# Decay exponents as products in PSUM: one change to a hybrid RG-LRU and gated-DeltaNet block on one core

## The chip, the cores and the metric

The kernel runs on one core of one Trainium2 chip. The core has a matrix engine (TensorE, PE in the profile), three engines for elementwise work (VectorE or DVE, ScalarE or ACT, GpSimd or POOL), and SyncE (SP), from whose queue this kernel issues its DMAs. Matrix products land in PSUM, eight banks of 128 partitions by 512 numbers of four bytes; everything else lies in SBUF, and large arrays in DRAM. The metric is device time in microseconds (us) of one execution, the median of several runs.

## The reference, cut to what matters

Two layers run over a context of 256 tokens and a latent stream of 256 tokens, with 1024 features. Layer 0 mixes with a bidirectional RG-LRU, layer 1 with a bidirectional gated DeltaNet; each is followed by a SwiGLU feed-forward part. The change lies in the DeltaNet. It has 8 query and key heads, 16 value heads of 128 numbers each, and two directions. Per chunk of tokens, head and direction it computes:

```python
gc = jnp.cumsum(gc, axis=-1)
diff = gc[..., :, None] - gc[..., None, :]
decay = jnp.where(incl, jnp.exp(jnp.where(incl, diff, 0.0)), 0.0)
kb = kc * bc[..., None]
m = jnp.where(strict, jnp.einsum('bhid,bhjd->bhij', kb, kc) * decay, 0.0)
rhs = jnp.concatenate([vc * bc[..., None], kb * jnp.exp(gc)[..., None]], axis=-1)
sol = lax.linalg.triangular_solve(m, rhs, left_side=True, lower=True, unit_diagonal=True)
u, w = sol[..., :d_v], sol[..., d_v:]
v_new = u - jnp.einsum('bhcd,bhde->bhce', w, s)
attn = jnp.where(incl, jnp.einsum('bhid,bhjd->bhij', qc, kc) * decay, 0.0)
o = (jnp.einsum('bhcd,bhde->bhce', qc * jnp.exp(gc)[..., None], s)
     + jnp.einsum('bhij,bhje->bhie', attn, v_new))
g_last = gc[..., -1]
s = (s * jnp.exp(g_last)[..., None, None]
     + jnp.einsum('bhcd,bhce->bhde', kc * jnp.exp(g_last[..., None] - gc)[..., None], v_new))
```

`q` and `k` are normalised per token and head, `beta` (`bc`) is a sigmoid, `g` a negative softplus. The kernel uses chunks of 128 tokens where the reference uses 64; the result of the recurrence doesn't depend on that.

## The kernel before

**An order made by a planner.** The kernel's text is not the order in which engines work. A `Recorder` takes every operation with a cost (`_cost`), the engines that could do it, and the tiles it reads and writes. `flush` then plays the engines forward by these costs: of what is ready it takes the lowest priority number (place in the text plus a `bias` for its stage), gives out buffers first in, first out, puts an operation with two possible engines on the one that ends it first, and issues the operations in that order. So all instructions carry line 576, the one that calls them, and groups of the profile are told apart by their tiles. Each engine then works strictly in the order it was given.

**Products.** A weight comes as a 128 by 1024 tile `raw` (3 buffers) by a DMA on SP. It is split into a rounded part `whi` and a rest `wlo` in the F32R type, and each product is three matmuls (`mm3`). Plain F32 matmuls show as two records each.

**The DeltaNet stages.** The 16 value heads go in four groups `g` of four value heads, that is two key heads. `TUNE["prog"]` lists the stages in order:

- A(h), `stage_a`: products for key, two value heads and query of head h; convolution (`cu`), SiLU, transposes, the norms `rk2`, spills of keys and values to DRAM.
- E(g), `stage_e`: the decays of a group in the tile `gn`: 32 matrices of 128 by 128, one for each of 4 chunks, 2 directions and 4 heads. One DMA of 2 MB broadcasts rows of the cumulated gates (`rows`, in DRAM) to all partitions; 8 selects on POOL put -1e30 or 1e30 on one side of the diagonal; 32 exponentials on ACT add the column's part as a bias.
- N(g), `stage_n`: `gn` times minus beta (`nbt`), times the products of keys with keys (`ps_g`), and then the inverses of the 32 by 32 diagonal blocks of all 32 matrices at once, on DVE (`lw`, `lmul`): 30 steps of two instructions and some transposes.
- L(g), `stage_l`: merging of the blocks' inverses to the inverse of 128 by 128, with matmuls of 32 rows (`ps_w1`, `ps_z`) and then of 64 (`ps_w2`, `ps_z2`), both kinds shown without their digit. Its `first` and `second` run over both directions and both halves: all of `first`, then all of `second`.
- P(g), `stage_p`: for each key head a broadcast `qg` of 0.5 MB, selects to `at`, exponentials of both, `at` times beta and the product of keys and queries (`ps_kq`), and `qg` times the query.
- C(g), `stage_c`: the recurrence over four chunks for both directions: `ps_ks`, `r`, `ps_y`, `yy`, `ps_s`, the state `S`, and in the last two steps the outputs `ps_o`, a sum of two products in PSUM (`qg` with `S`, `at` with `yy`), gathered in `oa`.
- Z and W: products for the output gate, gating, and the first part of the output projection.

PSUM is given out by tags: two banks `mm` for products, one `ta` for stage A, two `tr` for `ps_g`, `ps_kq` and all merges, three `st` for C. `gn` has two buffers, so E(g+2) waits for C(g).

Lines that matter: `PROG` and `TUNE` 72 to 74, `_cost` 259, `add_any` 321, `flush` 387, the gates' setup 1155 to 1201, E at 1272, N 1291, L 1344, `first` and `second` 1400 and 1412, P 1433, C 1480, the loop over the stages 1642.

## Time and profile before

| What | us |
|---|---|
| median of 3 runs (lowest, highest) | 1427.63 (1426.83, 1431.89) |
| the profiled execution | 1428.36 |
| its span, first to last instruction | 1426.6 |
| PE busy in it | 1308.5 |
| DVE busy | 1092.5 |
| ACT busy | 590.2 |
| POOL busy | 293.0 |
| DMA | 208.26 MB, a mean of 146 GB/s |

Layer 0 and its feed-forward part take the span up to some 640 us, the DeltaNet with its output projection the stretch to about 1205, and the last feed-forward part the rest. Busy time is the time in which an engine ran at least one instruction. Matmuls overlap, so the mean duration of one is longer than the distance to the next. The granted clock tells which share of TensorE's full clock it had.

### The profile page before, as it was taken

The numbers are of one execution on the slowest core, as the hardware profiler recorded it, in microseconds if no ns is written. First come the engines' busy times: TensorE is split into PE (matmuls) and PEld (weight loads), VectorE is DVE, ScalarE is ACT, GpSimd is POOL, SyncE is SP. The second block draws the span as 40 slices with busy tenths as digits, with TensorE's granted clock in tenths as the row PEclk, the third lists the DMA queues.
The fourth block names the chain that finished last, engine by engine and source line by source line (L and its number), as shares of the span: only waits on it lengthen the run. The fifth ranks groups of instructions, "written<-read, shape, count | busy, mean of one in ns | idle before, by whom it ended". The sixth has DMA issues, their size and how long they took to land.

```text
span 1426.6 us, 23481 instructions
## 1 busy us (share of the span) xinstructions
PE 1308.5 (92%) x9195; PEld 1126.8 (79%) x9195; DVE 1092.5 (77%) x1843; ACT 590.2 (41%) x1119; POOL 293.0 (21%) x273
## 2 busy tenths in 40 slices
PE   6999999899999999999868999799578899899997
PEld 3667768778888888897757889689577899899997
DVE  5889976777777776468699849869789777777775
ACT  3267863333334332025594453663543731211100
POOL 2000010100121110123566433623421320000000
PEclk9999999999999999999979979969669899899998
DMA  9544433355555554344752403603703215455563
GB/s 359 192 153 165 156 118 103 137 181 188 203 190 178 178 188 148 96 139 132 181 173 89 147 33 114 189 31 105 177 1 79 87 46 207 134 187 183 176 187 111
DMA packets 69791, 208.26 MB, mean 146 GB/s; under 512 B 6960, under 2 KB 14384, under 8 KB 69424
## 3 DMA queue, kind: packets, MB, share of 16 engines
q1 hardware_dynamic: 69680, 206.77, 45.7%
q8 instruction: 72, 1.18, 0.3%
q14 instruction: 39, 0.32, 0.1%
HBM read 196.71 MB, written 10.03 MB: 145 GB/s over the span
## 4 chain that ended last, share of the span: by engine, by line
PE 62%; issue 16%; DVE 11%; DMA 6%; ACT 3%; SPq 2%; POOL 0%; POOLq 0%; DVEq 0%; ACTq 0%
PE ps_mm L576 34%; PE ps_dn L576 9%; PE ps_g L576 4%; PE ps_ada L576 3%; PE ps_wo L576 2%; PE ps_z L576 2%; PE ps_o L576 2%; SPq L576 2%; PE ps_y L576 2%; DVE lw L576 2%; PE ps_w L576 2%; DVE cu L576 2%; DMA raw<-dn_w_in 1%; DMA spill<-on 1%; DMA kspill<-k 1%
## 5 line engine op out<-in xcount | busy, mean ns | idle before, releaser
L576 PE MATMUL ps_mm<-hh,whi 128*128 128x512 f32 (+1 forms) x888 | 330.8, 373 | 14.3 <-DVE cu L576 7.8
L576 PE MATMUL ps_mm<-hh,wlo 128*128 128x512 f32 (+1 forms) x888 | 327.1, 369 | 6.7 <-DVE wlo L576 4.6
L576 PE MATMUL ps_mm<-hl,whi 128*128 128x512 f32 (+1 forms) x888 | 326.2, 368 | 2.0 <-DVE hl L576 2.0
L576 DVE TENSOR_TENSOR wlo<-raw,whi 128x1024 fp32r<-128x1024 f32 (+2 forms) x189 | 233.3, 1234 | 26.4 <-ACT whi L576 18.3
L576 DVE CAST whi<-raw 128x1024 fp32r<-128x1024 f32 (+1 forms) x168 | 115.2, 686 | 143.6 <-PE ps_mm L576 69.2
L576 PEld LDWEIGHTS ps_mm<-hh,whi 128*128 128x128 f32 x888 | 172.3, 194 | 50.6 <-issue 9.6
L576 PEld LDWEIGHTS ps_mm<-hh,wlo 128*128 128x128 f32 x888 | 171.9, 194 | 36.1 <-DVE wlo L576 6.3
L576 PEld LDWEIGHTS ps_mm<-hl,whi 128*128 128x128 f32 x888 | 172.1, 194 | 26.6 <-DVE hl L576 2.2
L576 POOL TENSOR_TENSOR wlo<-raw,whi 128x1024 fp32r<-128x1024 f32 x49 | 118.7, 2423 | 234.5 <-ACT whi L576 101.4
L576 PE MATMUL ps_dn<-fh,whi 128*128 128x256 f32 (+1 forms) x374 | 122.7, 328 | 0.0
L576 PE MATMUL ps_dn<-fl,whi 128*128 128x256 f32 (+1 forms) x374 | 122.5, 328 | 0.0
L576 PE MATMUL ps_dn<-fh,wlo 128*128 128x256 f32 (+1 forms) x374 | 122.3, 327 | 0.0
L576 PE MATMUL ps_mm<-h2h,whi 128*128 128x256 f32 x352 | 100.8, 287 | 1.1 <-ACT h2h L576 1.1
L576 PE MATMUL ps_mm<-h2h,wlo 128*128 128x256 f32 x352 | 100.7, 286 | 0.4 <-DVE wlo L576 0.4
L576 PE MATMUL ps_mm<-h2l,whi 128*128 128x256 f32 x352 | 100.7, 287 | 0.0
L576 ACT ACTIVATE whi<-raw 128x1024 fp32r<-128x1024 f32 (+1 forms) x70 | 71.6, 1023 | 66.4 <-PE ps_mm L576 33.0
L576 ACT ACTIVATE fh<-sg 128x256 fp32r<-128x256 f32 (+1 forms) x43 | 22.4, 522 | 143.4 <-DVE sg L576 142.0
L576 POOL TENSOR_TENSOR x<-x,ring 128x1024 f32<-128x1024 f32 x13 | 34.3, 2635 | 212.6 <-ACT ring L576 212.6
L576 PEld LDWEIGHTS ps_dn<-fh,whi 128*128 128x128 f32 x374 | 71.1, 190 | 6.8 <-issue 0.4
L576 PEld LDWEIGHTS ps_dn<-fh,wlo 128*128 128x128 f32 x374 | 71.1, 190 | 6.2 <-DVE wlo L576 0.2
L576 PEld LDWEIGHTS ps_dn<-fl,whi 128*128 128x128 f32 x374 | 71.1, 190 | 5.9
L576 DVE SCALAR_TENSOR_TENSOR cu<-ps_mm,sm,cu 128x510 f32<-128x510 f32 (+2 forms) x96 | 64.9, 678 | 8.8 <-ACT cu L576 6.7
(301 smaller groups left out, 2735.3 us busy)
## 6 DMA issues: line engine op xcount, KB each, us to landing
ring<-ada_w SPq DMA_DIRECT2D x96, 512.0 KB, 4.5
raw<-ffn_gu SPq DMA_DIRECT2D x88, 512.0 KB, 3.7
raw<-dn_w_in SPq DMA_DIRECT2D x49, 512.0 KB, 3.7
raw<-ffn_down SPq DMA_DIRECT2D x34, 512.0 KB, 3.6
raw<-rg_w_in SPq DMA_DIRECT2D x16, 512.0 KB, 3.7
gn<-rows SPq DMA_DIRECT2D x4, 2048.0 KB, 16.3
raw<-ffn_down SPq DMA_DIRECT2D x17, 384.0 KB, 3.3
raw<-dn_w_out SPq DMA_DIRECT2D x12, 512.0 KB, 3.9
```

The lines of the kernel that those rows point to most:

```text
L576: call(*[real(x) for x in args], **{n: real(v) for n, v in kw.items()})
```

## The change

Decays. The broadcasts, the selects and the multiplication by beta go. In their place, the exponent of a whole decay matrix is summed up in a PSUM bank by three F32R products, for four heads at once: a column part (cumulated gate of the column, with the logarithm of beta in it), a row part, and a triangle of -1e30. One exponential reads the bank and writes the decay. Numbers are split in an F32R part and a rest, which lie in different rows of the same product. `stage_e` does this for `gn`, `stage_p` for `at`; `stage_e` therefore needs beta and the norms of both key heads, which `stage_n` worked out before.

```diff
+    def exponents(g, c, d, sign, bound, col, to, name="ps_e"):
+        ps = bank("tr", name)
+        p4 = ps.rearrange("p (h i) -> p h i", h=4)
+        i = 4 * c + g
+        lhs, rhs, n = col
+        T.matmul(p4, lhs, rhs.rearrange("p (h o) -> p h o", o=1).to_broadcast([n, 4, 128]), start=True, stop=False, needs=to)
+        T.matmul(p4, own[sign][:, i:i + 1].to_broadcast([128, 128]), rows[d], start=False, stop=False)
+        lhs, rhs = (identr, below) if bound > 0 else (below, identr)
+        T.matmul(p4, lhs, rhs.rearrange("p (o i) -> p o i", o=1).to_broadcast([128, 4, 128]), start=False, stop=True)
+        return p4
...
     def stage_e(g):
-        sync.dma_start(out=gn.rearrange("p (a h) i -> p a (h i)", h=4),
-                          in_=rows.raw(4 * g * 128, [[0, 128], [16 * 128, 8], [1, 512]]))
-        for d in range(2):
-            for c in range(4):
-                e = gn[:, sidx(c, d, 0):sidx(c, d, 0) + 4, :]
-                G.affine_select(out=e, in_=e, pattern=[[0, 4], [1, 128]], compare_op=OP.is_ge, fill=(-1e30, 1e30)[d],
-                                base=0, channel_multiplier=-1)
...
-                    S.activation(e, e, AF.Exp, scale=(1.0, -1.0)[d], after=all_in,
-                                 bias=(ngc, gc)[d][:, c, d, 4 * g + hv:4 * g + hv + 1])
...
+        lb = small([128, 4, 2, 4], "lb")
+        V.tensor_scalar(lb, bt, 1e-37, None, OP.max)
+        S.activation(lb, lb, AF.Ln)
...
+        for c in range(4):
+            for d in range(2):
+                s = sidx(c, d, 0)
+                p4 = exponents(g, c, d, (1, -1)[d], 1, column(t, c, d), [gn])
+                S.activation(gn[:, s:s + 4, :], p4, AF.Exp)
```

In `stage_n` the product with `ps_g` now carries the sign and works on half the columns, and the matmuls of `ps_g` (as those of `ps_kq` in `stage_p`) wait for all decays of their tile:

```diff
-                R.tt(g5[:, c, d], g5[:, c, d], nbt[:, c, d].rearrange("p (h o) -> p h o", o=1).to_broadcast([128, 4, 128]),
-                     OP.mult)
...
                 T.matmul(pg[:, 128 * c:128 * c + 128], kT[:, 128 * c:128 * c + 128], kT[:, 128 * c:128 * c + 128],
-                         start=True, stop=True)
+                         start=True, stop=True, after=decays)
...
+                for d in range(2):
+                    e = g5[:, c, d, 2 * q:2 * q + 2, :]
+                    V.scalar_tensor_tensor(e, pg[:, 128 * c:128 * c + 128].rearrange("p (a i) -> p a i", a=1)
+                                           .to_broadcast([128, 2, 128]), -1.0, e, OP.mult, OP.mult)
```

Queries. `qg` goes. In the last two steps of `stage_c` the plain query is multiplied with the state (`ps_qs`, 256 columns at once), and the decay `egq` is applied to the result on its way out of PSUM; the other product (`at` with `yy`) is added to it:

```diff
+                        T.matmul(pq[:, 256 * d:256 * d + 256], A[2 * g + q]["qT"][:, 128 * c:128 * c + 128], S0[q][:, d],
+                                 start=True, stop=True)
+                        for j in range(2):
+                            o, eg = oa[q][:, c, j], egq[:, c, d, 4 * g + 2 * q + j:4 * g + 2 * q + j + 1]
+                            if i == 2:
+                                S.activation(o, four(pq)[:, d, j], AF.Copy, scale=eg)
+                            else:
+                                V.scalar_tensor_tensor(o, four(pq)[:, d, j], eg, o, OP.mult, OP.add)
...
-                            T.matmul(p, qg[q][:, cs2[d] - 2, d, j], S0[q][:, d, j], start=True, stop=False)
-                            T.matmul(p, at[q][:, cs2[d] - 2, d, j], y[q][:, d, j], start=False, stop=True)
+                            T.matmul(p, at[q][:, cs2[d] - 2, d, j], y[q][:, d, j], start=True, stop=True)
```

Merges. `first` and `second` become generators, and `first` of direction 1 alternates, matmul by matmul, with `second` of direction 0:

```diff
-        for f in (first, second):
-            for d, half in items:
-                f(d, half)
+        for half in range(2):
+            list(first(0, half))
+        for half in range(2):
+            list(zip(first(1, half), second(0, half), strict=True))
+        for half in range(2):
+            list(second(1, half))
```

Planner. The order of the stages and the biases are new:

```diff
-PROG = "A0 E0 A1 N0 A2 A3 A4 E1 P0 L0 C0 N1 A5 L1 E2 N2 P1 C1 A6 L2 A7 Z0 P2 C2 Z1 Z2 E3 Z3 N3 L3 W0 P3 C3"
+PROG = "A0 A1 E0 A2 N0 A3 E1 L0 P0 N1 C0 A4 A5 E2 P1 L1 N2 C1 A6 Z0 A7 E3 L2 P2 N3 Z1 C2 Z2 Z3 L3 W0 P3 C3"
```

Five rules of `flush` and `_cost` change, and hold for the whole kernel, not for the DeltaNet alone: an F32R matmul is priced at `max(w / 2.4 + 13, 118)` ns in place of `max(w / 2.4, 54) + 2`; matmuls of 64 columns get a new price, less where two that use different halves of the array follow each other; DVE's time counts one and a half times where ACT could do the same; the `tr` banks are given to the tile that is asked for first, not in the order of the text (`loose`); and where the full-size matmuls of the current interval of 3.4 us fall short, a full-size matmul that is ready goes ahead of a narrow one (`warm`). The logarithm is added to the list of table sets.

The setup before the stages gains the constants of the products (`below`, `identr`, `pick`, `npick`, `own`, the split rows), some 20 small instructions, and loses the store of `rows` to DRAM.

More of the change, by code (lines that the diff above doesn't have):

```diff
@@ L350, in add_any @@
         op.narrow = eng == "PE" and ins[0].free() <= 32
+        op.group = None
+        if eng == "PE" and 32 < ins[0].free() <= 64 and ins[0].dt != F32R:
+            op.group = [int(x.sh.flat[0] >= x.t.sh.size // 4) for x in (ins[0], out)]
         op.cols = 0
@@ L355, in add_any @@
         deps = set(after)
-        op.tiles = list(dict.fromkeys(x.t for x in outs + ins))
+        op.tiles = sorted(dict.fromkeys(x.t for x in outs + ins + list(needs)), key=lambda t: t.psum)
         for x in ins:
@@ L419, in flush @@
                         fifo.setdefault(t.key, []).append(t)
-        waiting = {}
+        waiting, idle = {}, {}
+        loose = {t.key for op in ops for t in op.tiles if t.psum and t.tag in self.loose}
         engines = ["PE", "DVE", "ACT", "POOL", "SP"]
@@ L431, in offer @@
                     waiting.setdefault(t, []).append(op)
+                    if t.key in loose and free[t.key] > 0:
+                        grant(t.key, idle.get(t.key, 0.0))
                     return
@@ L439, in grant @@
             while q and free[key] > 0:
-                t = q.pop(0)
+                if loose and key in loose:
+                    asked = [t for t in q if t in waiting]
+                    if not asked:
+                        return
+                    t = min(asked, key=lambda t: (max(now, min(op.ready for op in waiting[t])), min(op.prio for op in waiting[t])))
+                    q.remove(t)
+                else:
+                    t = q.pop(0)
                 free[key] -= 1
@@ L451, in flush @@
         dma_free, table, done, held = 0.0, 1, 0, {}
-        at_tick, columns, slow, rows, narrow = 0, 0.0, False, 1, False
+        at_tick, columns, slow, rows, narrow, group = 0, 0.0, False, 1, False, None
         order = []
@@ L480, in flush @@
             cost, tab = op.alts[e][:2]
-            if e == "PE" and op.rows != rows:
+            warm = False
+            if e == "PE" and op.cols < cost:
+                if int(clock[e] / self.TICK) != at_tick or columns < self.TICK_COLUMNS:
+                    full = [x for x in avail[e] if x[0] < p + TUNE["warm"] and ops[x[1] - base].fin is None
+                            and ops[x[1] - base].cols >= ops[x[1] - base].alts[e][0]]
+                    if full:
+                        heapq.heappush(avail[e], (p, i))
+                        p, i = min(full)
+                        avail[e].remove((p, i))
+                        heapq.heapify(avail[e])
+                        op = ops[i - base]
+                        cost, tab = op.alts[e][:2]
+                        warm = True
+                        if op.rows != rows:
+                            cost += 106
+            if e == "PE" and op.rows != rows and not warm:
                 same = [x for x in avail[e] if ops[x[1] - base].rows == rows and x[0] < p + TUNE["stay"][rows == 1]]
@@ L496, in flush @@
                 narrow = op.narrow
+                if op.group and group and op.group[0] != group[0] and op.group[1] != group[1]:
+                    cost -= 53
+                    group = None
+                else:
+                    group = op.group
             def bank_free(op, e):
@@ L510, in flush @@
             if len(op.alts) > 1:
-                other = min((max(clock[x], bt, bank_free(op, x)) + op.alts[x][0], x) for x in op.alts if x != e)
-                if other[0] < max(clock[e], wait) + cost and not (avail[other[1]] and avail[other[1]][0] < (p, i)):
+                other = min((max(clock[x], bt, bank_free(op, x)) + op.alts[x][0] * (1.5 if x == 'DVE' and 'ACT' in op.alts else 1), x) for x in op.alts if x != e)
+                if other[0] < max(clock[e], wait) + cost * (1.5 if e == 'DVE' and 'ACT' in op.alts else 1) and not (avail[other[1]] and avail[other[1]][0] < (p, i)):
                     heapq.heappush(fut[e], (max(other[0] - cost, bt + 50), p, i))
@@ L566, in flush @@
                     free[t.key] += 1
-                    grant(t.key, t.last + (220 if t.psum else 130))
+                    idle[t.key] = t.last + (220 if t.psum else 130)
+                    grant(t.key, idle[t.key])
         self.log.append((max(clock.values()), dict(clock)))
@@ new lines, in hybrid_block @@
+    V.tensor_reduce(out=mod4, in_=ident.rearrange("p (m h) -> p h m", h=4), axis=AX.X, op=OP.add)
+    own = {}
+    for sign in (1, -1):
+        own[sign] = dn.tile([128, 16], F32R, name=f"own{sign + 1}")
+        t = piece(16)
+        V.tensor_reduce(out=t, in_=id64.rearrange("p (i h) -> p i h", h=4), axis=AX.X, op=OP.add)
+        V.tensor_scalar(own[sign], t, float(sign), None, OP.mult)
+    gch = dn.tile([128, 2, 2, 4, 16], F32R, name="gch")
+    for d in range(2):
+        R.copy(gch[:, d, 0], gc[:, :, d, :])
+        V.tensor_tensor(gch[:, d, 1], gc[:, :, d, :], gch[:, d, 0].bitcast(F32), OP.subtract)
@@ L1360, in stage_l @@
                 for a, b in ((0, 1), (2, 3)):
[L1361 removed]
+                    T.matmul(ps[B[b], o:o + 32], gn[B[a], s, B[b]], dt[B[a], s, :], start=True, stop=True, needs=[w1])
             for b in (1, 3):
@@ L1397, in stage_l @@
         G.memset(g5[B[2], :, 1, :, B[3]], 0.0)
-        w2s, items = {}, [(d, half) for d in range(2) for half in range(2)]
+        w2s = {}
         def first(d, half):
```

156 lines of the change are left out of this document (82 added, 74 removed).

## Prediction

> **What bounds the kernel now.** I read the page first: its row of granted clock, and its chain of work that ended last.
>
> ```profile
> PEclk9999999999999999999979979969669899899998
> PE 62%; issue 16%; DVE 11%; DMA 6%; ACT 3%; SPq 2%; POOL 0%; POOLq 0%; DVEq 0%; ACTq 0%
> ```
>
> The clock row is at or near 9 until the middle of the span and sags only in the third quarter. The chain is mostly PE, but DVE, DMA and the SP queue (SPq) share a fifth of it. So there are stages with different limits. The view of busy time by stretches, cut around the DeltaNet stage, gives:
>
> ```profile
> 0.00:640.00 640.00, 615.42 (x3120) 483.20 (x3121) 472.52 (x665) 264.42 (x376) 77.60 (x64) 0.99 0.51 170
> 640.00:688.00 48.00, 44.78 (x261) 37.72 (x260) 38.78 (x91) 30.11 (x62) 18.30 (x15) 1.00 0.47 151
> 688.00:1205.00 517.00, 440.03 (x4129) 399.88 (x4128) 419.30 (x855) 268.29 (x618) 195.70 (x193) 0.87 0.38 109
> ```
>
> The numbers in a row are length, then busy time and count of PE, weight loads, DVE, ACT and POOL, then clock, DMA share and GB/s. Up to 640 us PE is busy for 615 of 640 us at clock 0.99: nothing that the change does there can gain more than about 25 us. The 517 us from 688 on are another matter. PE is busy for 440 us of them at clock 0.87, which is 440 x 0.87 = 383 us of work at full clock (an estimate). So 134 us are lost there: 77 us of idle PE and 57 us of slowed PE. DVE, at 419 us, is nearly as full. PE work, DVE work and the waits between them set this stage together.
>
> The same view in pieces of 20 us shows where the 134 us lie:
>
> ```profile
> 700.00:720.00 20.00, 10.04 (x47) 8.01 (x46) 12.12 (x19) 13.32 (x36) 9.23 (x14) 0.80 1.01 204
> 720.00:740.00 20.00, 13.71 (x60) 11.26 (x60) 17.37 (x28) 17.15 (x51) 14.99 (x15) 0.69 0.46 169
> 920.00:940.00 20.00, 13.59 (x365) 12.66 (x364) 18.38 (x26) 19.77 (x52) 10.76 (x11) 0.59 0.31 105
> 940.00:960.00 20.00, 19.48 (x156) 18.41 (x155) 10.84 (x18) 10.26 (x22) 3.84 (x7) 0.64 0.01 1
> 1000.00:1020.00 20.00, 10.16 (x68) 9.34 (x66) 16.77 (x34) 5.22 (x12) 7.42 (x11) 0.81 0.97 188
> 1020.00:1040.00 20.00, 13.75 (x378) 13.39 (x379) 14.35 (x28) 17.56 (x42) 6.18 (x10) 0.50 0.33 121
> 1040.00:1060.00 20.00, 19.28 (x139) 17.96 (x137) 15.15 (x24) 10.99 (x31) 6.01 (x10) 0.67 0.00 1
> 1060.00:1080.00 20.00, 10.99 (x61) 9.57 (x62) 19.65 (x50) 1.84 (x4) 3.43 (x6) 0.83 0.09 26
> ```
>
> Two kinds of loss can be told apart. At 700 and at 1000 us the DMA share is about 1 while PE idles half of the time. At 920 to 960 and 1020 to 1060 us the DMA is nearly quiet and the clock is between 0.50 and 0.67: there the merges of `stage_l` run, with matmuls of 32 and 64 rows. At 1060 us DVE is full and PE waits for it.
>
> What fills the DMA shows in the SP queue's timeline and in the list of DMA issues:
>
> ```profile
> 685.90 1.13 SPq L576 DMA_DIRECT2D gn<-rows  x2
> 687.08 13.26 SPq L576 DMA_DIRECT2D qg<-rows  x2
> 700.44 6.51 SPq L576 DMA_DIRECT2D kl<-kspill  x1
> 707.05 1.50 SPq L576 DMA_DIRECT2D raw<-dn_w_in  x1
> ...
> gn<-rows SPq DMA_DIRECT2D x4, 2048.0 KB, 16.3
> ...
> qg<-rows SPq DMA_DIRECT2D x8, 512.0 KB, 21.7
> ```
>
> The broadcasts of `rows` are 4 x 2 MB and 8 x 0.5 MB, 12 MB in all. Issuing two of the small ones holds SP for 13.26 us, so that the weights `raw` queued behind them are issued at 707.05. For some 20 us PE has no product to do.
>
> **The change part by part.** First the work, by durations of these groups (busy time in all, and mean of one in ns, after the bar):
>
> ```profile
> L576 ACT ACTIVATE gn<-gn,gc 128x128 f32<-128x128 f32 x64 | 21.0, 388 | 0.1
> L576 POOL TENSOR_SCALAR_AFFINE_SELECT gn<-gn 128x512 f32<-128x512 f32 x32 | 20.8, 679 | 13.9 <-DMA gn<-rows 13.9
> L576 ACT ACTIVATE gn<-gn,ngc 128x128 f32<-128x128 f32 x64 | 20.6, 388 | 0.1
> L576 ACT ACTIVATE at<-at,ngc 128x128 f32<-128x128 f32 x64 | 20.4, 390 | 0.2
> L576 DVE TENSOR_TENSOR gn<-ps_g,gn 128x512 f32<-128x512 f32 x32 | 19.9, 682 | 18.9 <-PE ps_g L576 18.7
> ...
> L576 ACT ACTIVATE yy<-ps_y 128x512 f32<-128x512 f32 x32 | 19.1, 596 | 62.4 <-PE ps_y L576 62.3
> ...
> L576 DVE TENSOR_TENSOR gn<-gn,nbt 128x512 f32<-128x512 f32 x24 | 17.5, 738 | 6.2 <-ACT gn L576 6.1
> ...
> L576 DVE SCALAR_TENSOR_TENSOR r<-ps_ks,nbc,vb 128x128 f32<-128x128 f32 x48 | 15.3, 340 | 0.0
> ...
> L576 ACT ACTIVATE vp<-ps_vt,nkh 128x128 f32<-128x128 f32 x44 | 12.7, 366 | 11.3 <-DMA kspill<-k 6.0 <-PE ps_vt L576 2.8 <-DVE vp L576 1.2
> ...
> L576 POOL TENSOR_TENSOR qg<-qg,qT 128x512 f32<-128x512 f32 x9 | 12.0, 1349 | 4.7 <-ACT qg L576 4.7
> ...
> L576 DVE TENSOR_TENSOR oa<-ps_o,oa 128x256 f32<-128x256 f32 x16 | 6.6, 420 | 4.2 <-PE ps_o L576 4.2
> ...
> 341.10 42.19 PE ps_mm L576 x186
> ```
>
> *PE.* Each exponent tile is three products with 512 columns in F32R. Per group there are 8 tiles in `stage_e` and 4 in `stage_p`; with four groups that is 4 x 12 x 3 = 144. The last row shows such products back to back: 42.19 / 186 = 0.227 us. So 144 x 0.227 = **+32.7 us**, all counted on the path, since PE is the fullest engine. The query's product with the state costs PE the same as before: 32 of 256 columns in place of 64 of 128.
>
> *ACT.* It loses the 192 exponentials of 128 columns (21.0 + 20.6 + 20.4 us). It gains 32 of 512 columns at 0.596 us (19.1), 32 of 256 columns, which I put between 0.366 and 0.596, at 0.48 (15.4), and 32 scaled copies at 0.366 (11.7): some 16 us less. The logarithm is four small instructions.
>
> *POOL.* It loses the selects on `gn` (20.8) and its part of the query scaling (12.0), and what it had of the others.
>
> *DVE.* It loses the scaling of `gn` (17.5). The 32 of 512 columns on `ps_g` (682 ns) become 64 of 256 at about 0.42 (the `oa` row): 26.9 for 21.8. For the query it gains 32 at 0.340 (10.9) and 16 more adds at 0.420 (6.7). That is near zero in sum, with up to 8 us of small setup instructions more. But the planner now counts DVE time one and a half times where ACT can do the same, and ACT has 249 us idle in the stage. I take **-10 us** for what leaves DVE and POOL, between +5 (only the setup is felt) and -30 (all the ACT and POOL time freed is used).
>
> *The broadcasts.* At 700 to 740 us PE loses 9.96 + 6.29 us idle and 10.04 x 0.20 + 13.71 x 0.31 = 6.3 us by the clock, 22.5 in all. At 1000 to 1040 us it is 9.84 + 6.25 + 8.8 = 24.9. The first goes whole, as its DMA share of 1.01 is that of the broadcasts. Of the second I take 15.5, since there the merges also wait for the inverse that DVE makes. Together **-38 us**, between -22.5 and -47.4. What is late next: `stage_e` now needs the key norms of both heads of its group, so the first exponentials wait for A1. The products on `ps_g` and `ps_kq` carry a new wait for all decays of their tile; PE works in order, and weights' products queued behind such a wait stand too. That is the price if the cover goes.
>
> *The merges.* The new order runs `first(1)` and `second(0)` in pairs. The trace has a few such pairs by chance:
>
> ```profile
> 937.38 0.41 PE L576 MATMUL ps_mm<-hh,whi 128*128 128x256 f32 x1
> 937.59 0.41 PE L576 MATMUL ps_mm<-hl,whi 128*128 128x256 f32 x1
> 938.05 1.97 PE L576 MATMUL ps_w<-xo,gn 64*64 64x64 f32 x16
> ...
> 943.77 0.31 PE L576 MATMUL ps_z<-gn,lw 64*64 64x64 f32 x1
> 943.82 0.31 PE L576 MATMUL ps_w<-gn 64*64 64x64 f32 x1
> 943.88 3.08 PE L576 MATMUL ps_z<-gn,lw 64*64 64x64 f32 x27
> ```
>
> Alternating, they start 0.05 to 0.06 us apart; alone, 3.08 / 27 = 0.114 us. Per group 64 records are paired, which saves about 64 x 0.057 = 3.6 us at this low clock and half of that at full clock: four groups give **-7 us** (to -14).
>
> *The planner's rule for the clock* (`warm`) puts full-size matmuls between narrow ones. The clock's loss at 920 to 960 and 1040 to 1060 us is 13.59 x 0.41 + 19.48 x 0.36 + 19.28 x 0.33 = 19 us. I take **-8 us**, between 0 and -19. Against it stands a row: from the last product at 937.59 to the narrow matmul at 938.05 it is 0.46 us, where products follow each other at 0.21, so a change of size costs about 0.25 us. [...]
>
> *The order.* N3 now stands before Z1 and C2, so the last inverse is made on DVE while C2 still runs. PE's 9.0 idle us at 1060 go: **-9 us**, between 0 and -11. N3 brings no DMA with it, and the broadcasts that E3 used to put on SP there are gone.
>
> *Elsewhere* the new prices only reorder; with 25 us of idle PE before 640 us I take 0, between +10 and -10.
>
> **Sum:** 32.7 - 10 - 38 - 7 - 8 - 9 = -39.3 us. The profiled execution took 1428.36 us, 1.8 us more than its span of 1426.6, and 0.7 us more than the median of 1427.63. So 1428.4 - 39.3 = **1389 us**.
>
> **The rivals.**
> *The losses go nearly whole.* The stage would then be PE work, 383 + 32.7 - 7 = 409 us, plus a third of today's 134 us: 454 us, 63 less, or 1365. For it: exponent products need neither weights nor DMA and can fill gaps. Against: DVE's 419 us are not shortened by that.
> *The stalls stay.* Three `raw` buffers and one SP queue hold back the weights anyway; the 38 us shrink to nothing: 1427, no change. Against: the DMA share of 1.01.
> *Changes of size.* Ten full products put into each of four merges cost 40 x 0.25 = 10 us, and the 8 us of clock are not won: 1407.
> *Slower: banks.* The exponents share the two `tr` banks with the merges. One tile holds its bank for 3 x 0.227 us of products and 0.596 us of exponential, 1.28 us. There are 12 merge tiles in a group, 48 in all; if each waits for one exponent tile, that adds 61 us: 1389 + 61 = 1450. It decides from 39.3 / 1.28 = 31 of the 48 on. For it: the merges' PE time is a chain. Against: the new planner hands `tr` banks to whoever is ready.
>
> **How the numbers follow.** Chances: forecast 0.44 (own range 1370 to 1408), losses go 0.25, changes of size 0.09, stalls stay 0.11, banks 0.11. A measurement of this kernel can tell about 0.5% from no change, 7 us. Faster by more: 0.44 + 0.25 + 0.09 and 0.02 of the stalls case, 0.80; within: 0.07; slower: 0.11 + 0.02 = 0.13. All unknown costs at their good ends give 32.7 - 30 - 47.4 - 14 - 19 - 11 - 10 = -99 us, at their bad ends 32.7 + 5 - 22.5 + 10 + 10 = +35; that all fall on one side is unlikely. The range leaves out the bank case and a little of the losses case: 1350 to 1430.
>
> **What would show it.** In the changed profile no `gn<-rows` and `qg<-rows`; no 20-us piece with PE at half and DMA at 1; `ps_e` and `ps_a` with 144 F32R products near 0.23 us apart, not waiting for banks; ACT and POOL each lower by tens of us in the stage; a stage of some 478 us with a clock over 0.87. I am wrong if PE's idle time stays near 77 us, if `ps_g` or `ps_kq` stands for long on `gn` or `at`, or if the clock in the merges stays at 0.5.

## The result, and the profile after

| | before | after |
|---|---|---|
| median, us (4 runs each, on one chip) | 1428.45 (1426.83 to 1431.89) | 1372.24 (1371.01 to 1377.74) |
| the profiled execution | 1428.36 | 1377.74 |
| its span | 1426.6 | 1376.0 |
| DMA, MB | 208.26 | 195.62 |

The ratio is 0.9611, with a 95% interval from 0.9578 to 0.9643. The forecast was 1389 us, in a range from 1350 to 1430. The profiled execution of the changed kernel is the longest of its four, 5.5 us above the median: what follows places 50.6 us of span, while the medians differ by 56.2.

Where the time went shows best when the span is cut at two marks that both kernels have: the last product of layer 0's feed-forward part (`ps_dn`), and the last product of the DeltaNet's output projection (`ps_wo`). First the view by stretches of the kernel before, in front of the stage and in it (columns as in the prediction: length, then busy time and count of PE, weight loads, DVE, ACT, POOL, then clock, DMA share, GB/s):

```profile
0.00:638.20 638.20, 614.01 (x3111) 482.01 (x3111) 470.77 (x660) 262.72 (x374) 76.24 (x64) 0.99 0.51 170
638.20:1215.20 577.00, 496.41 (x4483) 449.00 (x4484) 467.46 (x960) 300.61 (x684) 215.36 (x208) 0.88 0.39 113
```

The same of the changed kernel:

```profile
0.00:628.30 628.30, 612.54 (x3109) 481.14 (x3109) 481.84 (x655) 267.41 (x382) 75.42 (x64) 0.99 0.52 173
628.30:1165.60 537.30, 514.57 (x4569) 443.59 (x4568) 419.49 (x980) 298.15 (x634) 170.52 (x145) 0.95 0.29 98
```

Layer 0 is 9.9 us shorter, the DeltaNet 39.7, and what follows 1.0 (211.4 against 210.4): 50.6 us of span. Inside the stage PE idles for 537.3 - 514.6 = 22.7 us, where it was 577.0 - 496.4 = 80.6. The slowed clock costs 514.6 x 0.05 = 26 us, where it was 496.4 x 0.12 = 60. So some 92 us of losses went, but PE's own work grew: at full clock it is 514.6 x 0.95 = 489 us against 496.4 x 0.88 = 437, 52 more. (The mean clock of a long window counts idle stretches too: in the run below with broadcasts that nothing reads, PE is busy for 0.00 us from 700 to 740 us, and the clock of both 20-us rows there is 0.50. Summed over 170 slices of some 3 us, the numbers are 58 us less idle time, 28 less by the clock and 46 more work.) DVE and POOL lost 48 and 45 us of busy time in the stage; ACT lost only 2.5.

In the page's chain of work that ended last, DVE has half of its former 11%, and the SP queue is gone from it:

```profile
PE 56%; issue 16%; DVE 6%; ACT 3%; DMA 1%; POOL 0%; POOLq 0%; SPq 0%; ACTq 0%; DVEq 0%
```

The pieces in which the kernel before stood are full; two are not. Of 20 us each, in the changed kernel:

```profile
720.00:740.00 20.00, 16.84 (x81) 13.77 (x80) 17.20 (x41) 8.59 (x24) 6.67 (x4) 0.83 0.30 102
1060.00:1080.00 20.00, 15.94 (x372) 14.44 (x371) 8.68 (x11) 12.54 (x25) 5.55 (x5) 0.55 0.21 68
1080.00:1100.00 20.00, 20.00 (x148) 17.96 (x148) 4.35 (x14) 5.94 (x10) 2.54 (x4) 0.59 0.00 1
```

At 720 us a little of the old hole is left; at 1000 us, where the second one was, PE is busy for 19.24 of 20 us. From 1060 to 1100 us the last merge, L3, runs at clock 0.55 and 0.59: in PE's timeline few products stand between its steps there (six of 256 columns, `ps_wo`, among the 148 matmuls from 1080 to 1100 us). What PE waits for in the stage (total, times, longest) is short now:

```profile
PE ps_mm L612 <- DVE cu L612: 5.6, 3, 3.2
PE ps_wo L612 <- POOL ol L612: 3.2, 2, 2.2
```

`ps_g`, `ps_kq` and the merges' `ps_w` are nowhere on that list.

### Where the 50 us of new PE work come from

The forecast priced an exponent tile at three products 0.227 us apart. PE's timeline of the changed kernel (start, busy us, instruction) shows a group of tiles at 690 us, and one of `stage_p`'s second direction at 930 us:

```profile
689.96 0.48 PE L612 MATMUL ps_e<-pick,cT 64*128 64x512 f32 x1
690.37 0.50 PE L612 MATMUL ps_e<-rows,own 128*128 128x512 f32 x1
690.70 0.40 PE L612 MATMUL ps_e<-below,identr 128*128 128x512 f32 x1
691.03 0.48 PE L612 MATMUL ps_e<-pick,cT 64*128 64x512 f32 x1
...
930.54 0.38 PE L612 MATMUL ps_a<-npick,rT 128*128 128x512 f32 x1
930.75 0.40 PE L612 MATMUL ps_a<-rows,own 128*128 128x512 f32 x1
930.99 0.39 PE L612 MATMUL ps_a<-identr,below 128*128 128x512 f32 x1
931.22 0.28 PE L612 MATMUL ps_mm<-hh,wlo 128*128 128x256 f32 x1
```

The second tile, all of 128 rows, takes 931.22 - 930.54 = 0.68 us, as priced. The first begins with the column part `pick,cT`, which has 64 rows, and takes 691.03 - 689.96 = 1.07 us: 0.41 + 0.33 + 0.33. Of 48 tiles 40 are of that kind (32 of `stage_e`, 8 of `stage_p`): 40 x 1.07 + 8 x 0.68 = 48 us, not 32.7 (an estimate from these two tiles). The pairs of the merges take about 7 us off again (below); so some 5 of the 46 us stay without a name.

### The profile page after: what moved, and what is told of

Its sections match the earlier page's. It is cut to its first block, busy times and chain, and to the rows that moved or that the text cites. A ratio compares the mean times of both kernels' runs of the same rounds, so it can differ in the third digit from the quotient of the medians.

```text
span 1376.0 us, 23471 instructions
## 1 busy us (share of the span) xinstructions
PE 1324.9 (96%) x9280; PEld 1120.7 (81%) x9280; DVE 1055.5 (77%) x1856; ACT 591.5 (43%) x1078; POOL 247.3 (18%) x210
## 2 busy tenths in 40 slices
DMA packets 61262, 195.62 MB, mean 142 GB/s; under 512 B 6752, under 2 KB 9952, under 8 KB 60896
## 4 chain that ended last, share of the span: by engine, by line
PE 56%; issue 16%; DVE 6%; ACT 3%; DMA 1%; POOL 0%; POOLq 0%; SPq 0%; ACTq 0%; DVEq 0%
PE ps_mm L612 28%; PE ps_dn L612 9%; PE ps_e L612 2%; PE ps_y L612 2%; PE ps_wo L612 2%; PE ps_z L612 2%; PE ps_w L612 2%; PE ps_s L612 2%; PE ps_ks L612 1%; DVE lw L612 1%; PE ps_a L612 1%; PE ps_qs L612 1%; DVE cu L612 1%; PE ps_o L612 1%; DMA ring<-ada_w 1%
## 5 line engine op out<-in xcount | busy, mean ns | idle before, releaser
L612 POOL TENSOR_TENSOR wlo<-raw,whi 128x1024 fp32r<-128x1024 f32 x53 | 127.1, 2399 | 356.3 <-DVE whi L612 193.4
L612 ACT ACTIVATE whi<-raw 128x1024 fp32r<-128x1024 f32 (+2 forms) x66 | 68.1, 1031 | 63.7 <-PE ps_mm L612 33.2
L612 ACT ACTIVATE ring<-ring,cs 128x1024 f32<-128x1024 f32 x42 | 48.3, 1150 | 64.4 <-DVE x L612 64.4
```

The lines of the kernel that those rows point to most:

```text
L612: call(*[real(x) for x in args], **{n: real(v) for n, v in kw.items()})
```

## The experiments

All runs are compared with the kernel before on the same chip; differences in the text are of medians, and by the ratios up to 4 us other. "Offsets" are the entries of `bias`, which move a stage's operations in the planner's priority. Each fence with a row of the view by stretches below is cut at the same two marks.

| run | us, median | ratio, 95% interval |
|---|---|---|
| planner rules alone | 1419.23 | 0.9931 [0.9901, 0.9961] |
| old decays, queries and merges; new rules, order, offsets | 1424.50 | 0.9976 [0.9944, 1.0009] |
| new decays, old order and offsets | 1444.95 | 1.0102 [1.0067, 1.0138] |
| new decays, old order, new offsets | 1408.77 | 0.9855 [0.9794, 0.9915] |
| new decays, new order, old offsets | 1426.53 | 0.9983 [0.9958, 1.0008] |
| without the clock rule | 1420.21 | 0.9935 [0.9911, 0.9958] |
| broadcasts put back | 1437.40 | 1.0044 [1.0019, 1.0069] |
| broadcasts that nothing reads | 1476.54 | 1.0314 [1.0267, 1.0362] |
| merges apart | 1382.50 | 0.9671 [0.9632, 0.9711] |
| N3 late | 1375.26 | 0.9605 [0.9557, 0.9654] |
| column part padded | 1366.89 | 0.9576 [0.9529, 0.9622] |
| padded, six offsets changed | 1357.80 | 0.9486 [0.9442, 0.9530] |

The theory after the result: the decays off the DMA make the gain, the rest is small. The rival: it is the planner, its rules or its order. Both fell: the rival with the first two runs, the theory with the third.

### The planner's rules alone, and with the new order and offsets

The first run is the kernel before, its `PROG` and offsets kept, with the new rules except `loose`, which names tiles that only the new text has:

```diff
-TUNE = dict(ev=3000, stay=(300, 0), ...
+TUNE = dict(warm=5000, ev=3000, stay=(300, 0), ...
...
-                return max(w / 2.4, 54) + 2
+                return max(w / 2.4 + 13, 118)
```

> The text and the order of before, with the new planner rules (prices of matmuls, DVE's time weighted, full-size matmuls ahead of narrow ones), without the rule for the tr banks. Theory 1 (the broadcasts cost most, the planner little): the some 10 us that layer 0 gained come, and at most 8 us in the DeltaNet stage: 1410 to 1418 us. Theory 2 (the new planner rules alone fill PE and keep its clock): 1380 to 1395 us.

The second run adds the new `PROG` and the new offsets to it; the decays, queries and merges stay the old ones.

> The decays, queries and merges of before, in the new order of stages with the new biases and the new planner rules (again without the rule for the tr banks). Theory 1: the broadcasts still hold SP and the DMA engines, so PE still idles for tens of us in the stage: 1400 to 1415 us. Theory 2 (order and planner make the gain): 1375 to 1390 us.

The rules alone give 1419.23 us, just above the first theory's 1410 to 1418. Their view by stretches, in front of the stage and in it:

```profile
0.00:624.00 624.00, 605.17 (x3109) 477.37 (x3109) 478.89 (x655) 267.38 (x382) 75.85 (x64) 0.99 0.52 174
624.00:1205.40 581.40, 496.25 (x4483) 444.43 (x4483) 455.68 (x942) 306.20 (x704) 215.13 (x203) 0.89 0.39 112
```

Layer 0 ends at 624.0 us, 14 earlier than before; the stage is not shorter (581.4 us, 85 of them idle, clock 0.89). So the gain ahead of the DeltaNet is the rules', and nothing else of theirs helps by itself. With the new order too it is 1424.5, a little above what both theories had. The SP queue's timeline, PE's longest wait, and the view by stretches around it:

```profile
673.74 12.82 SPq L612 DMA_DIRECT2D qg<-rows  x2
...
709.25 0.33 SPq L612 DMA_DIRECT2D kl<-kspill  x1
```

```profile
722.99 0.99 PE L612 MATMUL ps_ssq<-ones,sqq 128*128 128x1 f32 x4 [24.53 <-DVE lmul L612]
```

```profile
700.00:710.00 10.00, 0.00 (x0) 0.00 (x0) 10.00 (x14) 9.97 (x30) 8.78 (x11) 0.66 0.79 212
710.00:720.00 10.00, 0.00 (x0) 0.00 (x0) 9.92 (x10) 9.97 (x32) 1.97 (x3) 0.50 0.17 61
```

SP is held for 12.82 us at the two broadcasts of `qg`, and the reload `kl` comes at 709.25; but only POOL waits for that one, 3.5 us. While PE stands for 24.53 us, DVE and ACT are full: with the exponentials of single matrices, the scalings and products on `gn` and the transposes for the inverse. They come late: the broadcasts of `gn` are issued at 672.70, POOL's selects on the first start at 690.29, and those on the second wait for theirs until 699.16. PE's wait ends on a DVE instruction behind them. The hole is that of the old decays, transfer and elementwise work together, and the new order doesn't take it away.

### The decays alone, then order and offsets one at a time

These three are the changed kernel with its `PROG`, its offsets, or both, set back to those of before (with E0 behind A1, whose norms it needs). The offsets are:

```diff
-bias={'C3': -1500, 'N2': -300, 'N0': 100, 'L1': -300, 'N': -700, 'Z3': -1500, 'L': -1500, 'A3': 700, 'P0': 1500, 'A2': 300, 'E3': 700, 'E1': 1500, 'Z1': -100, 'W': 10000, 'P1': -700, 'C0': 0, 'L3': -1500, 'E': -300, 'A6': -100, 'W0': 10000, 'A7': -300, 'A4': -100, 'P': -100, 'E0': -300, 'N3': -700, 'P2': 0}
+bias={'C3': -1500, 'N0': 100, 'N': -700, 'Z3': -1200, 'L': -1500, 'E3': 700, 'W': 10000, 'L3': -800, 'E': -300, 'W0': 10000, 'P': -100, 'E0': -300, 'N3': -700, 'P2': 0, 'C': 400, 'A': 700, 'Z': 700, 'C1': 0}
```

> The new decays, queries and merges with all new planner rules, in the order and with the biases of before (E0 moved behind A1, which it now needs). Theory 1: most of the gain stays, and what the place of N3 was worth (9 us) and some tuning go: 1380 to 1392 us. Theory 2: the gain was in the order, 1400 us or more.

> New decays and new planner, the stages in the order of before (E0 behind A1), but with the changed kernel's offsets to the priorities. The run with the old order and the old offsets took 1444.95 us, the changed kernel 1372.24. If the offsets made the loss (the old ones put the exponents of group 1 1500 and of group 3 700 behind their place, so that they come as single tiles late), this run is near the changed kernel: 1370 to 1390. If the place of the stages in the text made it, it stays at 1430 to 1455. If both count, it lies between, 1390 to 1430.

> New decays, new planner and new order of the stages, with the old offsets to the priorities. By offsets alone: 1430 to 1455, and the exponential of single exponent tiles scattered over the stage. By the order alone: 1370 to 1390. By both: between.

The first of them is a plain miss for the theory: 1444.95 us, slower than before, with the broadcasts gone. The other two lie between it and the changed kernel, at 1408.77 and 1426.53: order and offsets both count. Both cost idle time, and the offsets clock besides. The stage with both old, with the old order, and with the old offsets:

```profile
623.60:1225.40 601.80, 528.97 (x4568) 459.69 (x4568) 434.05 (x1014) 304.56 (x628) 163.15 (x126) 0.90 0.26 88
```

```profile
624.00:1197.40 573.40, 517.09 (x4567) 445.23 (x4568) 431.86 (x985) 305.98 (x641) 161.43 (x137) 0.93 0.27 92
```

```profile
623.60:1213.80 590.20, 534.89 (x4569) 462.71 (x4568) 431.13 (x1004) 308.07 (x635) 167.66 (x130) 0.90 0.27 89
```

*The order* costs idle time, most of it at one place. With the old order the changed decays idle for 573.4 - 517.1 = 56.3 us, 33.6 more than the changed kernel, and 24 of them are one wait, that of the last group's merge for DVE's last inverse (in PE's timeline, the idle time before it in brackets; the run with both old has 24.48 us there):

```profile
1106.78 3.43 PE L612 MATMUL ps_w<-ldt,gn 32*32 32x32 f32 x121 [23.99 <-DVE ldt L612]
```

How late that inverse is shows in the row of `ldt`, the transposition that ends each of the four inverses (count, ns, first and last start), in the changed kernel, with the old order, and in the run with both old:

```profile
L612 DVE STREAM_TRANSPOSE ldt<-lw x4: 2043/2158/2234, 779.9 to 1062.1; 128x1024 f32<-128x1024 f32 x4
```

```profile
L612 DVE STREAM_TRANSPOSE ldt<-lw x4: 1904/2030/2135, 769.6 to 1104.7; 128x1024 f32<-128x1024 f32 x4
```

```profile
L612 DVE STREAM_TRANSPOSE ldt<-lw x4: 1918/1976/2173, 786.3 to 1132.2; 128x1024 f32<-128x1024 f32 x4
```

1062.1, 1104.7 and 1132.2 us. The row of the exponentials `gn<-ps_e` says why: the last one starts at 993.5, 1061.9 and 1084.2. In the old order E3 stands behind C2, Z1 and Z2; the new one has it before L2 and P2, and E3 brings no DMA. That this place alone makes the difference was not tried, and it is not enough: with the new order and the old offsets the last exponential starts at 1060.0 too, though E3's own offset is 700 in both lists.

*The offsets* cost as much idle time: 590.2 - 534.9 = 55.3 us, 32.6 more than the changed kernel. It lies in more places; the longest wait is again that for the last inverse:

```profile
1122.97 2.26 PE L612 MATMUL ps_w<-ldt,gn 32*32 32x32 f32 x77 [10.35 <-DVE ldt L612]
```

They cost clock, too. With the old ones PE is busy for 534.9 us at clock 0.90, where the changed kernel has 514.6 at 0.95. Summed over slices, as above, the slowed clock costs 44.5 us with the old offsets, 23.0 in the changed kernel, and 23.2 with the old order, whose mean of 0.93 is low by its idle time alone. The merge at 1120 us in the run with the old offsets:

```profile
1120.00:1140.00 20.00, 15.23 (x391) 14.44 (x392) 4.91 (x7) 13.27 (x27) 1.12 (x3) 0.50 0.01 3
```

The new offsets put all of A and, but for Z3, of Z, the stages of full-size products, 700 behind their place. That they leave these products for the merges fits the clock in the three runs (a loss of 23.2 us with the new offsets and the old order, of 44.5 and 42.2 with the old offsets), but which of the entries does it was not tried one by one.

### Without the clock rule

```diff
-            if e == "PE" and op.cols < cost:
+            if False and e == "PE" and op.cols < cost:
```

> The changed kernel without the planner's rule that puts full-size matmuls ahead of narrow ones. If that rule is what keeps the clock up in the merges, their half clock comes back: up to 20 us, 1380 to 1392 us, with a clock near 0.9 in the stage. If the clock is up because PE no longer idles before and between the merges, the time stays within 5 us: 1368 to 1377 us.

It took 1420.21 us, far above the 1380 to 1392 expected: one rule of the planner carries 48 us, six times the term of the forecast. The stage, and the piece with the last merge:

```profile
629.10:1212.80 583.70, 534.96 (x4569) 461.22 (x4567) 423.36 (x974) 307.53 (x648) 173.96 (x141) 0.92 0.27 90
1120.00:1140.00 20.00, 20.00 (x186) 18.11 (x179) 0.85 (x2) 7.37 (x15) 0.95 (x1) 0.50 0.01 2
```

The full-clock work is the same as in the changed kernel (535.0 x 0.92 = 492 against 489 us): what goes is clock, 17 us (22 by the slices), and idle time, 48.7 us in place of 22.7. The idle time is the less obvious half. The likely reading is that a merge without products between its steps runs slowly (from 780 to 800 us, in the first one, the clock is 0.59, with the rule 1.00), ends later, and what hangs on it comes later: the last `ldt` starts at 1109.1 us, not 1062.1.

How the rule works shows in the first merge of the changed kernel, at full clock:

```profile
786.20 0.40 PE L612 MATMUL ps_mm<-hh,whi 128*128 128x512 f32 x1
786.53 0.31 PE L612 MATMUL ps_w<-ldt,gn 32*32 32x32 f32 x8
786.77 0.50 PE L612 MATMUL ps_mm<-hl,whi 128*128 128x512 f32 x1
787.11 0.40 PE L612 MATMUL ps_mm<-hh,wlo 128*128 128x512 f32 x1
```

From the last product before the narrow matmuls to the first of them it is 0.33 us, from the first product behind them to the next again 0.34, where like products stood 0.22 to 0.24 apart above: a change of size costs 0.10 us here, not the 0.25 us that the forecast read from a row at half clock (0.50 from 936 to 940 us in the kernel before). The row at 1120 us shows that a busy PE alone does not keep the clock up in this kernel: PE is busy for all of 20.00 us there, and the clock is 0.50. What runs in such a stretch shows in the last merge of the changed kernel, from 1080 to 1095 us: PE is busy for 15.00 of 15 us at clock 0.50, 92 of its 118 matmuls have 64 rows, and up to 1094.1 us those of 128 rows come in four bursts of 0.9 to 2.0 us. From 780 to 800 us, with 36 full-size products between the steps of the first merge, the clock is 1.00 and PE is busy for 19.96 us.

### The broadcasts back, and broadcasts that nobody waits for

The first run is the changed kernel that also broadcasts rows into `gn` and `at`, 12 MB as before, and then overwrites them with the exponentials. In the second the same transfers, from the same places of the text, go to areas in DRAM that nothing reads. `rowsd` is a copy of the rows in DRAM, written once in the setup of both.

```diff
+        sync.dma_start(out=gn.rearrange("p (a h) i -> p a (h i)", h=4),
+                       in_=rowsd.raw(4 * g * 128, [[0, 128], [16 * 128, 8], [1, 512]]))
...
+        for q in range(2):
+            sync.dma_start(out=t["at"][q].rearrange("p c d h i -> p (c d) (h i)"),
+                           in_=rowsd.raw((4 * 16 + 4 * g + 2 * q) * 128, [[0, 128], [16 * 128, 4], [1, 256]]))
```

```diff
+        gd = dr.tile([128, 32, 128], F32, name=f"gd{g}")
+        sync.dma_start(out=gd.rearrange("p (a h) i -> p a (h i)", h=4),
...
+            qd = dr.tile([128, 2, 2, 2, 128], F32, name=f"qd{2 * g + q}")
+            sync.dma_start(out=qd.rearrange("p c d h i -> p (c d) (h i)"),
```

> The changed kernel with the broadcasts of before put back as transfers: 4 x 2 MB into gn ahead of the exponentials, 8 x 0.5 MB into at, then overwritten. The arithmetic stays that of the changed kernel. Theory 1 (traffic and the hold of SP are the loss): 25 to 45 us more, 1397 to 1417 us, with pieces of 20 us in which DMA is near 1 and PE idles. Theory 2 (the new order would have hidden the transfers; the selects, scalings and exponentials of before were the cost): at most 8 us more, up to 1380 us.

> The changed kernel with the 12 MB of broadcasts issued at their old places, but written to a scratch area in DRAM that nothing reads, so that no engine waits for them. With them written into gn and at, and overwritten, the time was 1437.4 us, 65 us over the changed kernel. If the traffic and the SP queue's issuing make the loss, this run is at 1420 to 1440. If the wait of the exponentials and the products behind them on the transfer makes it, this run is at 1372 to 1390; between 1390 and 1420 both have a share. Of the 65 us I expect less than half to be left: 1395.

Put back, they cost 65 us (1437.40), more than the 25 to 45 expected; the stage has 62.8 us idle and clock 0.90:

```profile
626.60:1226.70 600.10, 537.34 (x4568) 461.13 (x4568) 432.74 (x998) 294.75 (x631) 152.80 (x130) 0.90 0.37 109
```

The longest of the waits is PE's for an exponential on ACT that stands for its transfer:

```profile
713.02 0.66 ACT L612 ACTIVATE at<-ps_a 128x256 f32<-128x256 f32 x2 [5.69 <-DMA at<-rowsd]
713.46 0.42 PE L612 MATMUL ps_cb<-ident,cb 128*64 128x128 f32 x1 [16.44 <-ACT at L612]
```

Where nobody waits for them they cost 104 us (1476.54), well over what any of the theories had. Nothing holds them back, so that all four of `gd` and all eight of `qd` are issued one behind the other, from 677 to 743 us. In order of time, the SP queue, DVE, and PE of that run:

```profile
678.49 17.67 SPq L612 DMA_DIRECT2D qd<-rowsd  x2
...
704.15 22.81 SPq L612 DMA_DIRECT2D qd<-rowsd  x4
...
751.27 3.28 SPq L612 DMA_DIRECT2D kl<-kspill  x1
```

```profile
771.34 0.42 DVE L612 TENSOR_TENSOR kw<-kl,wc 128x256 f32<-128x256 f32 x1 [81.83 <-DMA kl<-kspill]
771.69 0.60 DVE L612 TENSOR_TENSOR cb<-lb,cb 128x32 fp32r<-128x32 f32 x1
```

```profile
772.43 0.39 PE L612 MATMUL ps_cb<-ident,cb 128*64 128x128 f32 x1 [82.01 <-DVE cb L612]
```

The reload `kl` stands behind the broadcasts on SP, is issued at 751.27, and lands 20.1 us later, where its median in the changed kernel is 2.8. DVE's `kw` waits for it, 81.83 us; behind `kw` stands `cb` on the same engine; PE's `ps_cb` waits for `cb`, and behind it the products: `ps_mm<-hl,whi` runs at 772.48, 0.05 us after `ps_cb`, though DVE, ACT and POOL were busy for 0.00 us from 700 to 760 us, so that what it reads had long been made. So no engine needs to wait for a broadcast: the one SP queue, on which the broadcasts are issued from 677.07 to 742.83, and engines that keep here to the order they were given pass the delay on. How much of it is SP's issuing and how much the traffic (DMA share 0.77 to 0.96 from 700 to 760 us) the run doesn't separate. This bunching is the run's own; it shows the mechanism, not the price in the kernel before.

### Merges apart, and N3 late

```diff
-        for half in range(2):
-            list(first(0, half))
-        for half in range(2):
-            list(zip(first(1, half), second(0, half), strict=True))
-        for half in range(2):
-            list(second(1, half))
+        for f in (first, second):
+            for d in range(2):
+                for half in range(2):
+                    list(f(d, half))
```

> The changed kernel with first and second of the merges one after the other, as before. If the pairs save PE time on the path, 3 to 7 us more at full clock: 1375 to 1380 us. If the merges lie beside products that fill PE anyway, no change beyond reordering: 1368 to 1376 us.

```diff
-PROG = "... E3 L2 P2 N3 Z1 C2 Z2 Z3 L3 W0 P3 C3"
+PROG = "... E3 L2 P2 Z1 C2 Z2 Z3 N3 L3 W0 P3 C3"
```

> The changed kernel with N3 put back behind Z3, where it was before. In the kernel with the new decays and the old order PE stood 24.5 us for the last inverse. If the place of N3 is what that order lacked, that wait comes here too: 9 to 25 us more, 1381 to 1397 us. If it was the old biases or other stages, the time stays within 5 us.

The merges apart take 1382.50 us, 10 more than the changed kernel and 2 above the 1375 to 1380 expected. By the slices, PE's work at full clock in the stage is 498.5 us there and 491.6 in the changed kernel: the pairs save 6.9. N3 late takes 1375.26, which its interval can't tell from the changed kernel's. Its last `ldt` shows why:

```profile
L612 DVE STREAM_TRANSPOSE ldt<-lw x4: 2098/2164/2259, 777.3 to 1062.5; 128x1024 f32<-128x1024 f32 x4
```

1062.5 us, as in the changed kernel: N3 becomes ready when E3 is done, and its offset of -700 takes it to the front wherever it stands in the text.

### The column part padded, and more offsets

The first of these fills the rows 64 to 127 of `cT` and `pick` with zeros, so that all three products of a tile have 128 rows. The second changes six offsets on top of that (its expectation counts seven).

```diff
+    G.memset(pick[64:128].bitcast(F32), 0.0)
...
+        G.memset(cT[64:128].bitcast(F32), 0.0)
...
-        return t["cT"][0:64], pick[0:64, 4 * (2 * c + d):4 * (2 * c + d) + 4], 64
+        return t["cT"], pick[:, 4 * (2 * c + d):4 * (2 * c + d) + 4], 128
```

> The changed kernel, with the column part of the exponents padded with zeros from 64 to 128 rows. In its trace an exponent tile whose column part has 64 rows takes 1.07 us of PE, one with 128 rows 0.69 us; 40 of the 48 tiles are of the first kind, so some 15 us of PE are at stake. If PE is what bounds the stage now, 8 to 15 us go: 1357 to 1364 us. If those tiles lie in time that PE has free, nothing changes beyond what a new order of instructions brings: 1368 to 1376 us.

```diff
-'N0': 100, ... 'C1': 0})
+'N0': 500, ... 'C1': 1500, 'A7': 2200, 'A1': 1100, 'C0': 1900, 'A3': -800})
```

> The version with the column part padded to 128 rows (1366.89 us), with seven more offsets to the priorities (all of C0, C1, A1 and A7 later, A3 earlier, N0 a little later). If what is left of idle time, 34 us with 7.05 us of it at 998, hangs on the order in which ready work is taken, this gains 5 to 15 us: 1352 to 1362. If it hangs on DVE, which is busy for four fifths of the stage, the time stays at 1363 to 1372.

Padded, PE's timeline has the three products of a tile evenly apart:

```profile
691.18 0.38 PE L612 MATMUL ps_e<-pick,cT 128*128 128x512 f32 x1
691.40 0.39 PE L612 MATMUL ps_e<-rows,own 128*128 128x512 f32 x1
691.63 0.39 PE L612 MATMUL ps_e<-below,identr 128*128 128x512 f32 x1
```

The time is 1366.89 us, 5 less than the changed kernel, where 8 to 15 less were expected; their intervals overlap, so the gain in time is not clear of noise. The work at full clock fell by about 13 us (496.2 busy at clock 0.96, 476 us; 9 by the slices), and idle time rose by 11, as the row shows:

```profile
624.40:1154.80 530.40, 496.19 (x4570) 438.89 (x4568) 433.89 (x998) 296.81 (x626) 173.50 (x149) 0.96 0.30 99
```

With the six offsets it is 1357.80 us, 0.9486 of before, and beats both kernels. The stage, and its last inverse:

```profile
624.10:1142.00 517.90, 493.12 (x4570) 437.66 (x4568) 428.64 (x989) 300.01 (x636) 162.90 (x140) 0.97 0.30 102
```

```profile
L612 DVE STREAM_TRANSPOSE ldt<-lw x4: 2085/2166/2209, 793.3 to 1031.7; 128x1024 f32<-128x1024 f32 x4
```

The last `ldt` starts at 1031.7, 30 us earlier than in the changed kernel, and the idle time is back at 24.8 us though DVE is busy for four fifths of the stage: that part of it hung on the order, not on DVE.

## Why the prediction was right, and where only its sum was

The time came out in the forecast's range, 17 us below the forecast: the medians differ by 56 us where 39.3 were forecast. In the profiled execution the stage shrank by 39.7 us. That agreement is luck, two errors that cancel. The forecast had 25.7 us of new PE work (32.7 less 7) and 65 us of losses gone; the runs have about 50 and 90. The state reached is that of the rival "the losses go nearly whole", in which a third of the losses stays, with an exponent product half again as dear.

- *Exponent products, +32.7.* Mis-sized: 48 us, since 40 of 48 tiles change between 64 and 128 rows. The step that failed took the distance of like products (0.227 us) for products of two kinds. The sign "products near 0.23 us apart" held for 8 tiles of 48. The forecast weighed a price for a change of size, the 0.25 us of one row, on the merges only. Such a change bears on the exponents too: where the padded run took the one between 64 and 128 rows away, the extra 0.39 us of a tile went (1.07 to 0.68).
- *DVE and POOL, -10.* POOL fell by 45 us and DVE by 48, more than reckoned. ACT did not fall by tens of us: it lost 2.5. Work went from DVE to it (in the stage ACT has 41 copies `gn<-ps_z` for 26, and 24 `lw<-ps_w` for 18), and its table loads rose in the stage (busy, mean ns), before and after:

```profile
L576 ACT ACT_TABLE_LOAD x23 | 29.5, 1283 | 3.3 <-DVE zs L576 2.2 <-DVE cu L576 0.8
```

```profile
L612 ACT ACT_TABLE_LOAD x33 | 42.3, 1283 | 1.7 <-DVE cu L612 1.2
```

Ten more, 12.8 us; the forecast called the logarithm four small instructions and left out its tables. Each of the four has a load right before it (680.88, 747.96, 828.42 and 966.21 us); what made the other six is not shown. On ACT it cost nothing that shows. What this term is worth in time by itself was not measured.

- *Broadcasts, -38.* That they cost PE its time held, but the step by which they do was read too narrowly. The forecast had PE without products because weights stand behind the broadcasts on SP. In the kernel before, the longest wait in the first hole is another one:

```profile
721.89 2.08 PE L576 MATMUL ps_kq<-qT,kT 128*128 128x128 f32 x8 [11.85 <-DVE gn L576]
```

PE waits for the work of the decays themselves: the first `gn` reaches POOL's selects at 701.84, ACT's 32 exponentials of it run from 709.26 to 718.7, and DVE's products follow. Transfer and elementwise work both went with the change, so this term holds both, and how they share it was not measured. Put back into the new kernel, the transfers alone cost 65 us, over the upper bound of 47.4. The bound counted only the pieces in which PE stood; in that run the last inverse also comes 50 us later (1111.9).
- *Merges in pairs, -7.* Right: 6.9 us of PE work, and 10 us of time by the run, with intervals of some 5 us on each side.
- *The clock rule, -8.* The mechanism held (the stage's clock is 0.95 with the rule, 0.92 without), its size did not: 48 us. The step that failed bounded the gain by the clock lost in the merges' pieces (19 us). Of the 48 us, 26 were idle time, which the bound didn't count. The rival "changes of size" fell with it, at 0.10 us a change.
- *N3's place, -9.* PE's wait at 1060 us did go, but not by N3's place in the text, which changes nothing with the new offsets. The last inverse starts early where E3's exponentials do (993.5), and that takes the new order, the new offsets and the missing broadcast together: with any one of them taken back the last exponential starts at 1056.8 or later (without the clock rule at 1031.8).
- *Elsewhere, 0.* 11 us, just past the bound: the new rules close up layer 0.
- *Banks.* That rival fell: among PE's waits in the stage the merges have one of 2.4 us (`ps_z`) and no other of a microsecond.

What the sum could not show is that its terms are no terms. Taken out alone, the clock rule is worth 48 us, the removed broadcasts 65, the offsets 54 and the order 37, of a total of 56. Put into the kernel before (ratios times 1428), the rules alone give 10 us, the rules with the new order and offsets 3, and the rules with the new decays, queries and merges lose 15. Each is needed by the others. As the runs read, one chain of four inverses goes through the stage, and PE is full only when every one of them comes in time and finds products to stand beside its merge. Among kernels with the new decays the last `ldt` marks the stage: it starts at 1031.7, 1045.9, 1062.1, 1104.7, 1109.1, 1120.9 and 1132.2 us in the runs of 1357.80, 1366.89, 1372.24, 1408.77, 1420.21, 1426.53 and 1444.95, and the stage ends 93 to 110 us behind it. With the broadcasts back it is 1111.9 and 1437.40, out of that row; and so are the kernels with the old decays (1104.5 in the kernel before, 1095.5 with the rules alone, 1090.9 with the new order too, at 1428.45, 1419.23 and 1424.50). That it sets the end is shown only where PE stands and waits for it. One reservation stays open: each variant was run with priorities tuned for another one, so a part's worth holds for these priorities. What the old decays would reach with offsets fitted to the new rules was not tried, and six offsets alone were worth 9 us (13 by the ratios).

## What to carry to other kernels

Where a stage is a chain with full-size work beside it, bound a change not by the pieces in which the engine stands today, but also by what comes later when a piece runs slow; and expect parts that feed one schedule not to add up. Before pricing small products that are put between others, look for a row in which such a change of shape happens at the same clock (here it cost 0.25 us at clock 0.50 and 0.10 at 1.00); zero rows that keep the shape can be cheaper than fewer rows (here 0.68 us a tile in place of 1.07). Where one queue issues all loads, look at what stands behind a large transfer, and behind what waits for that, whether or not anybody reads it: here DVE and PE stood for 82 us with `kl` behind broadcasts that nothing reads. And take the wait to be priced from the row of the engine that stands: here that row named `gn`, not the weights.

## What the hardware showed that was not expected

- A product of 64 rows among products of 128 rows, 512 columns each, is followed at 0.41 us, and its two neighbours at 0.33 (changed kernel, 689.96), where 128-row products stand 0.23 us apart (930.54). Padded with zero rows, all three are at 0.21 to 0.23 (691.18).
- PE was busy for 20.00 of 20 us at a clock of 0.50 (1120 us, without the clock rule), and for 15.00 of 15 us at 0.50 with 92 of 118 matmuls of 64 rows (1080 us, changed kernel). Without the clock rule the first merge has 0.73 and 0.59 from 760 to 800 us (PE busy for 11.91 and 19.24 us); with full-size products between its steps it runs at 1.00 in the changed kernel (780 to 800 us, PE busy for 19.96).
- SP is held for 12.82 us by two broadcasts of 0.5 MB (673.74, old decays in the new order) and for 17.67 and 22.81 us by two and by four (678.49 and 704.15, broadcasts that nothing reads), some 6 to 9 us each, where other broadcasts were issued just before. Two of 2 MB each, issued right before 673.74 with no broadcast ahead of them, took 1.00 us. So the 1.00 us of that issue said little of what came behind it; whether the issuing or the transfers ahead hold SP no run separates. The reload `kl` is issued in a third of a microsecond at 709.25.
